# Layer norms that sum their squares on TensorE, and closings that share the low parts of their weights among three engines: one change to a two-block fp32 kernel

## The chip, the cores and the metric

One Trainium2 chip, one of its cores. Five engines work side by side, each through its own queue and in order: TensorE (PE in the profile, its weight loads as PEld), VectorE (DVE), ScalarE (ACT), GpSimd (POOL) and SyncE (SP, which only issues DMAs). The metric is the device time of one execution in microseconds (us). Sequence 512, model width 1024, everything float32.

## The reference

Two blocks of two layers run one after the other. The first block: a convolution module (`conv`) and an FFN (`ffn0`), a sparse attention (`nsa`) and an FFN (`ffn1`). The second: a state-space mixer (`mamba`) and an MLP (`mlp0`), a stick-breaking attention (`sb`) and an MLP (`mlp1`). What the change touches is the layer norm inside the convolution module and the four of the second block:

```python
def layer_norm(x, g, b):
    mu = jnp.mean(xf, axis=-1, keepdims=True)
    var = jnp.mean(jnp.square(xf - mu), axis=-1, keepdims=True)
    return ((xf - mu) * lax.rsqrt(var + LN_EPS) * g + b)
...
h = layer_norm(DEEPNORM_ALPHA * h + mix, ln_mix_g[layer], ln_mix_b[layer])
h = layer_norm(DEEPNORM_ALPHA * h + squared_relu_mlp(h, mlp_w1[layer], mlp_w2[layer]), ...)
```

## The kernel before, in words

Activations lie feature-major: a tile `x[m]` (m = 0 to 7) holds 128 features by 512 tokens. Every float32 product is made of three matmuls (`mm3`, lines 135 to 137): weights and activations are split into a high part that the fast matmul type represents, and a low part, the rest. So each weight that arrives by an SP DMA (`wraw`) has to be split before PE can use it (`w`, lines 108 to 133): ACT writes the high part `whi`, and the low part `wlo` comes in one of three ways, chosen by `c.weng`: a subtraction on DVE (`None`) or on POOL (`nc.gpsimd`), both at line 96, or `"dma"`: ACT writes minus the high part (L122) and a DMA issued from POOL adds the raw weight to it (L123).

Five weight slots are turned over in order: weight n takes the buffers of weight n-5, so it can be loaded and split only when PE is through with that one.

A **closing** (`closing` and `out_halves`) ends `mamba`, `mlp0`, `sb` and `mlp1`. It runs the out-projection twice, over tokens 0 to 255 (half 0) and 256 to 511 (half 1), with eight weights each time. DVE adds each result to `x` (L523) and sums the features (`add`, L312 and L314). The layer norm is `HalfNorm`, once for each half, in three stages:

- `centre`: PE adds up the features over the partitions (L319), DVE subtracts the mean (L323), ACT squares (L328), and DVE adds the squares up in two sums (L329, six adds for a half).
- `stats`: four one-column matmuls (L336) sum each half of 128 tokens over the partitions. DVE turns the sums into 1/sqrt (`rstd_of`, L152 to L162).
- `finish`: PE spreads the result over the partitions (L183, two matmuls). DVE multiplies (L538), ACT adds the bias and writes the high part of the next product's activations (L540), DVE their low part (L543).

The three stages of half 0 are issued among the products of half 1's out-projection; those of half 1 among the first products of the next phase, the `head`: 4 or 5 weights of 128x1024, split at the end of the closing. `mlp1` ends the kernel: it has no head, and its half 1 is a chain with nothing beside it. The convolution's layer norm uses the same class, and its out-projection takes its low parts by turns from DVE and POOL.

In all closings `c.weng` is POOL, for the eight weights of both halves (128x512 in `mamba` and `sb`, 128x1024 in `mlp0` and `mlp1`) and for the head.

The order of the work is not that of the program text. The class `Arrange` takes all instructions, their dependences and a price for each, and lists them greedily: at each step the instruction that can start first, ties by a priority (the table `PRIO` moves some groups up or down). What comes out is the fixed order of each engine's queue. `graph` builds the dependences, `price` and `schedule` hold the costs.

Of the kernel before, what the change touches and what calls it, by code (L numbers as in the profile page):

```python
# [11 lines left out]
AF = mybir.ActivationFunctionType  # L12
OP = mybir.AluOpType
AX = mybir.AxisListType
PSUM = bass.MemoryType.PSUM
P = 128
S = 512
D = 1024
# [277 lines left out]
class HalfNorm:  # L296
# [19 lines left out]
    def centre(self, h):  # L316
        c, nc, cl = self.c, self.c.nc, self.cols(h)
        mu = c.bank()[:, :S // 2]
        nc.tensor.matmul(mu, c.ones, self.tot[h], start=True, stop=True)  # L319
        self.sq = acc = [c.s()[:, :S // 2] for _ in range(2)]  # L320
        for m in range(KT):
            y = self.ys[m][:, cl]
            nc.vector.scalar_tensor_tensor(y, mu, -1.0 / D, y, op0=OP.mult, op1=OP.add)  # L323
            if m < 2:
                nc.scalar.activation(acc[m], y, AF.Square)
            else:
                q = c.s()[:, :S // 2]
                nc.scalar.activation(q, y, AF.Square)  # L328
                nc.vector.tensor_tensor(acc[m % 2], acc[m % 2], q, op=OP.add)  # L329

    def stats(self, h):
        c = self.c
        ps = c.bank()
        for i in range(2):
            for j in range(2):
                c.nc.tensor.matmul(ps[:, i:i + 1], self.sq[j][:, i * P:(i + 1) * P], c.ones[:, :1], start=j == 0, stop=j == 1)  # L336
        self.r[h] = c.rstd_of(ps[:, :2], D, 1e-5)

    def finish(self, h):
        rs = self.c.rstd_spread(self.r[h], self.c.bank)[:, :S // 2]  # L340
# [169 lines left out]
    return [wl_(np.ascontiguousarray(w[a * P:b * P])) for a, b in ((0, 8), (8, 15), (15, 22))]  # L510


def out_halves(c, wname, hs, piece, beside, done=None):

    nc = c.nc
    for h in range(2):
        cl = slice(h * (S // 2), (h + 1) * (S // 2))
        ht = [[t[:, cl] for t in a] for a in hs]
        for m in range(KT):
            wt = c.w(c.ins[wname][piece][m])  # L520
            ps = c.t(c.pmm, [P, S], F32, "mm")[:, :S // 2]
            c.proj(ps, wt, ht)
            nc.vector.tensor_tensor(c.x[m][:, cl], c.x[m][:, cl], ps, op=OP.add)  # L523
            if done is not None:
                done(m, h)
            if (h, m) in beside:
                beside[h, m]()


def closing(c, wname, hs, piece, name, head):  # L530

    nc = c.nc
    c.weng = nc.gpsimd
    xs = c.acts() if head else None

    def apply(m, cl, rs):
        x = c.x[m][:, cl]
        nc.vector.scalar_tensor_tensor(x, x, c.pcol(name + "g", m), rs, op0=OP.mult, op1=OP.mult)  # L538
        if head:
            nc.scalar.activation(xs[0][m][:, cl], x, AF.Identity, bias=c.pcol(name + "b", m))  # L540
        nc.scalar.activation(x, x, AF.Identity, bias=c.pcol(name + "b", m))
        if head:
            nc.vector.tensor_tensor(xs[1][m][:, cl], x, xs[0][m][:, cl].bitcast(F32), op=OP.subtract)  # L543
        else:
            nc.sync.dma_start(c.ins["out"][m][:, cl], x)

    ln = HalfNorm(c, c.x, apply)
    s0, s1 = ln.stages(0), ln.stages(1)
    p = (0, 2, 4) if len(hs[0]) == KT else (0, 5, 7)
    out_halves(c, wname, hs, piece, {(1, m): f for m, f in zip(p, s0)}, ln.add)  # L550
    if not head:
        for f in s1:
            f()
        c.stored = True
        return
    wts = [c.w(src) for src in head]
    c.weng = None
    c.xs, c.head = xs, [c.t(c.pmm, [P, S], F32, "mm") for _ in head]
    for h in range(2):
        cl = ln.cols(h)  # L560
        for js in [(0, 1)] + [(j,) for j in range(2, len(head))]:
            for k in range(KT):
                for j in js:
                    sl = slice(k * P, k * P + P)
                    c.mm3(c.head[j][:, cl], wts[j][0][:, sl], wts[j][1][:, sl], xs[0][k][:, cl], xs[1][k][:, cl],
                          k == 0, k == KT - 1)
                if h == 0 and (js[0], k) in c.hpos:
                    s1.pop(0)()
# [1155 lines left out]
class Arrange:  # L1724
# [11 lines left out]
    def __init__(self, tc, edges=()):  # L1736
        self.tc, self.ins = tc, [i for b in tc.nc.cur_f.blocks if b.name == tc.start_bb_name for i in b.instructions]
        n = len(self.ins)
        self.eng, self.deps, self.touch = [-1] * n, [()] * n, [()] * n
        self.tag, self.bufs, self.count = {}, {}, {}  # L1740
        self.graph()
        at = {i.name: j for j, i in enumerate(self.ins)}
        for a, b in edges:
            self.deps[at[b]] = tuple(set(self.deps[at[b]]) | {at[a]})
        self.cost = [self.price(j) for j in range(n)]
        self.users, self.missing = [[] for _ in range(n)], [0] * n
        for j in range(n):
            for k in self.deps[j]:
                if self.eng[j] >= 0 and self.eng[k] >= 0:
                    self.users[k].append(j)  # L1750
                    self.missing[j] += 1
# [19 lines left out]
    def graph(self):  # L1771
        seen, closed, opened, gate, psum = {}, [], [], {}, set()
        for j, i in enumerate(self.ins):
# [29 lines left out]
            for nm, w, b in here:  # L1803
                d.update(k for k, w2, b2 in seen.get(nm, ()) if (w or w2) and (b2[0] < b[1] and b[0] < b2[1] and b2[2] < b[3] and b[2] < b2[3]
                                                                               or w and w2 and self.eng[j] == self.eng[k] == self.PE))
                if nm in psum:

                    d.update(k for k, w2, b2 in seen.get(nm, ()) if self.eng[j] != self.eng[k] and b2[2] < b[3] and b[2] < b2[3])
                if nm in gate:
                    d.add(gate[nm])  # L1810
            for nm, w, b in here:
# [8 lines left out]
    def price(self, j):  # L1820

        i, e = self.ins[j], self.eng[j]
        if e in (-1, self.GATE):
            return 0, 0, False
        kind = type(i).__name__
        if kind == "InstLoadActFuncSet":
            return 1283, 1283, False
        if kind == "InstDMACopy":
            return (870 if e == self.POOL else 370), 0, False
        size = lambda a: int(np.prod([n for _, n in list(a.ap)[1:]] or [1]))  # L1830
        mem = lambda a: self.tile(a) and ("P" if "PSUM" in str(self.tile(a).space) else "S")
        n = max(size(a) for a in list(i.ins) + list(i.outs) if hasattr(a, "ap"))
        if e == self.PE:
            n = size(i.ins[0])
            if i.is_transpose:
                o = 108
            elif "float32r" in str(i.ins[0].dtype):
                o = max(n / 2.4 + 12.7, 110) + 100 * (list(i.ins[1].ap)[-1][0] == 0)
            else:
                o = 2 * max(n / 1.2 + 12.7, 107)  # L1840
            return o, o + 165, False
        src = [mem(a) for a in i.ins if hasattr(a, "bass_ap") and mem(a) and (size(a) > 1 or n == 1)]
        if e == self.ACT:
            ptr = sum(1 for a in list(i.ins)[1:] if mem(a))
            d = (160 if mem(i.ins[0]) == "P" else 205) + 0.835 * n + (0, 75, 170)[min(ptr, 2)]
            return (d + 60, d + 30, False) if len(i.outs) > 1 else (d - 100, d, False)
        if e == self.DVE:
            fast = kind in ("InstTensorScalarPtr", "InstTensorCopy") and "P" not in src and len(src) < 2
            if kind == "InstMemset":
                d = 58 + 0.83 * n  # L1850
            elif fast:
                d = 150 + 0.54 * n
            elif kind == "InstReciprocal":
                d = 150 + 6.2 * n
            else:
                d = 150 + 1.05 * n + 45 * (kind == "InstTensorScalarPtr" and len(src) > 1 and len(i.ins) > 2)
            return d - 80, d, src.count("S") > 1 or fast
        d = {"InstMemset": 90 + 0.85 * n, "InstTensorScalarAffineSelect": 180 + 0.88 * n, "InstTensorCopy": 180 + 0.84 * n}.get(kind, 190 + 2.17 * n)
        return d - 50, d, kind != "InstMemset"
# [11 lines left out]
    def schedule(self, prio):  # L1871
# [12 lines left out]
        def release(j, end):  # L1884
            todo = [(j, end)]
            while todo:
                j, end = todo.pop()
                for u in self.users[j]:
                    ready[u] = max(ready[u], end + self.hop(self.eng[j], self.eng[u], type(self.ins[u]).__name__ == "InstDMACopy") if self.eng[j] != self.PE or self.eng[u] != self.PE else 0)
                    missing[u] -= 1  # L1890
                    if not missing[u]:
                        if self.eng[u] == self.GATE:
# [22 lines left out]
        for _ in range(sum(0 <= e < 5 for e in self.eng)):  # L1915
# [18 lines left out]
            if e == self.ACT:  # L1934
# [3 lines left out]
                    table = {"ln"}  # L1938
                elif f is not None:
                    if table is None or not table & set(f):  # L1940
                        start, table = start + 1283, set(f)
                    table = table & set(f)
            elif e == self.PE:
                w = int(start // 3413)
# [170 lines left out]
```

## Time and profile before

| what | value |
|---|---|
| median of 3 runs | 2956.26 us (2954.11 to 2956.95) |
| profiled execution | 2953.39 us |
| its span in the trace | 2951.6 us, mean granted PE clock 0.973 |
| HBM read | 246.33 MB, 84 GB/s over the span |

The profiled execution is one run of the program with the hardware profiler on; 1.79 us of it lie outside the span of the trace. It stands 2.87 us under the median of the three runs. Times in the trace count from the start of the span. A matmul of three parts on 256 tokens shows as three records, one for each of L135, L136 and L137; a full float32 matmul, as the one-column ones are, as two records.

### The profile page before, as it was taken

The numbers are of one execution on the slowest core, as the hardware profiler recorded it, in microseconds if no ns is written. First come the engines' busy times: TensorE is split into PE (matmuls) and PEld (weight loads), VectorE is DVE, ScalarE is ACT, GpSimd is POOL, SyncE is SP. The second block draws the span as 40 slices with busy tenths as digits, with TensorE's granted clock in tenths as the row PEclk, the third lists the DMA queues.
The fourth block names the chain that finished last, engine by engine and source line by source line (L and its number), as shares of the span: only waits on it lengthen the run. The fifth ranks groups of instructions, "written<-read, shape, count | busy, mean of one in ns | idle before, by whom it ended". The sixth has DMA issues, their size and how long they took to land.

```text
span 2951.6 us, 38106 instructions
## 1 busy us (share of the span) xinstructions
PE 2808.2 (95%) x14645; PEld 2390.0 (81%) x14645; DVE 1717.2 (58%) x2944; ACT 1489.2 (50%) x2317; POOL 453.1 (15%) x433
## 2 busy tenths in 40 slices
PE   8989999999888899999999999799999999799997
PEld 7878888878777688887788888688888888788887
DVE  8976344546877944444775756743336566743335
ACT  4454222336566632223886877443334788543333
POOL 0010000034222100000111111400015222500004
PEclk9989999998999999999999999899999999899998
DMA  5323323221111122233556564433333444423332
GB/s 189 122 80 124 100 89 103 86 71 53 46 46 45 42 95 93 93 101 105 140 129 143 126 160 107 129 100 100 93 99 115 115 121 91 140 93 94 99 93 93
DMA packets 94789, 300.18 MB, mean 102 GB/s; under 512 B 11216, under 2 KB 13776, under 8 KB 94608
## 3 DMA queue, kind: packets, MB, share of 16 engines
q1 hardware_dynamic: 80064, 253.58, 27.4%
q0 software_dynamic: 14544, 44.18, 7.9%
q8 instruction: 115, 1.88, 0.3%
q14 instruction: 66, 0.54, 0.1%
HBM read 246.33 MB, written 2.10 MB: 84 GB/s over the span
## 4 chain that ended last, share of the span: by engine, by line
PE 59%; ACT 4%; DVE 3%; issue 1%; DMA 1%; POOL 0%; ACTq 0%; POOLq 0%
PE mm L135 17%; PE mm L136 17%; PE mm L137 17%; PE z L1653 1%; PE e L1417 1%; DVE s L329 1%; DMA wlo<-wraw 1%; PE mm L1669 1%; PE e L1384 0%; PE e L1383 0%; ACT th L95 0%; PE mm L1027 0%; PE mm L1041 0%; DVE x L538 0%; ACT whi L121 0%
## 5 line engine op out<-in xcount | busy, mean ns | idle before, releaser
L95 ACT ACTIVATE whi<-wraw 128x1024 fp32r<-128x1024 f32 (+2 forms) x383 | 385.0, 1009 | 994.8 <-PE mm L136 780.4
L135 PE MATMUL mm<-xh,whi 128*128 128x512 f32 (+1 forms) x2240 | 847.8, 383 | 24.8 <-ACT whi L95 12.8
L137 PE MATMUL mm<-xh,wlo 128*128 128x512 f32 (+1 forms) x2240 | 848.9, 380 | 2.3 <-DVE wlo L96 1.4
L136 PE MATMUL mm<-xl,whi 128*128 128x512 f32 (+1 forms) x2240 | 848.8, 381 | 0.9 <-DVE xl L543 0.6
L135 PEld LDWEIGHTS mm<-xh,whi 128*128 128x128 f32 x2240 | 424.0, 191 | 106.4 <-ACT whi L95 15.4
L137 PEld LDWEIGHTS mm<-xh,wlo 128*128 128x128 f32 x2240 | 425.0, 190 | 83.5 <-DVE wlo L96 3.1
L136 PEld LDWEIGHTS mm<-xl,whi 128*128 128x128 f32 x2240 | 425.5, 190 | 79.0 <-DVE xl L543 1.7
L135 PE MATMUL mm<-hh,whi 128*128 128x512 f32 (+1 forms) x1344 | 482.8, 361 | 6.0 <-ACT whi L95 3.2
L137 PE MATMUL mm<-hh,wlo 128*128 128x512 f32 (+1 forms) x1344 | 482.2, 360 | 2.0 <-DMA wlo<-wraw 0.9
L136 PE MATMUL mm<-hl,whi 128*128 128x512 f32 (+1 forms) x1344 | 481.9, 360 | 0.9 <-DVE hl L96 0.9
L96 POOL TENSOR_TENSOR wlo<-wraw,whi 128x1024 fp32r<-128x1024 f32 (+2 forms) x119 | 255.9, 2160 | 1366.8 <-ACT whi L95 1348.8
L96 DVE TENSOR_TENSOR wlo<-wraw,whi 128x1024 fp32r<-128x1024 f32 (+1 forms) x264 | 316.3, 1200 | 183.7 <-ACT whi L95 180.8
L135 PEld LDWEIGHTS mm<-hh,whi 128*128 128x128 f32 x1344 | 255.2, 190 | 44.1 <-ACT hh L95 3.8
L137 PEld LDWEIGHTS mm<-hh,wlo 128*128 128x128 f32 x1344 | 255.1, 190 | 40.1 <-DMA wlo<-wraw 2.1
L136 PEld LDWEIGHTS mm<-hl,whi 128*128 128x128 f32 x1344 | 255.3, 190 | 36.9 <-DVE hl L96 1.4
L287 DVE TENSOR_TENSOR x<-x,mm 128x512 f32<-128x512 f32 x80 | 55.0, 687 | 222.5 <-PE mm L137 222.5
L123 POOL DMA_DIRECT2D wlo<-wraw x101 | 87.8, 870 | 518.7 <-ACT wlo L122 353.9
L121 ACT ACTIVATE whi<-wraw 128x1024 fp32r<-128x1024 f32 (+2 forms) x101 | 92.2, 913 | 87.0 <-PE mm L136 73.7
L96 DVE TENSOR_TENSOR hl<-s,hh 128x512 fp32r<-128x512 f32 (+1 forms) x120 | 88.0, 734 | 77.2 <-ACT hh L95 77.1
L503 DVE TENSOR_TENSOR s<-mm,rstd 128x512 f32<-128x512 f32 x44 | 30.4, 691 | 136.0 <-PE mm L137 136.0
L95 ACT ACTIVATE hh<-s 128x512 fp32r<-128x512 f32 (+1 forms) x120 | 75.8, 632 | 42.1 <-DVE s L504 27.9
L122 ACT ACTIVATE wlo<-wraw 128x1024 fp32r<-128x1024 f32 (+2 forms) x101 | 91.7, 908 | 5.8 <-PE mm L136 5.5
(454 smaller groups left out, 4101.7 us busy)
## 6 DMA issues: line engine op xcount, KB each, us to landing
wraw<-mlp_w SPq DMA_DIRECT2D x144, 512.0 KB
wraw<-ffn_w_in SPq DMA_DIRECT2D x88, 512.0 KB
wlo<-wraw POOLq DMA_DIRECT2D x68, 512.0 KB, 4.8
wraw<-ssm_w_in SPq DMA_DIRECT2D x48, 512.0 KB
wraw<-ffn_w_out SPq DMA_DIRECT2D x32, 448.0 KB
wraw<-conv_taps SPq DMA_DIRECT2D x20, 512.0 KB
wraw<-ssm_w_out SPq DMA_DIRECT2D x40, 256.0 KB
wraw<-conv_w_out SPq DMA_DIRECT2D x16, 512.0 KB
```

Of the source, the lines that this page charges most:

```text
L95: nc.scalar.activation(hi, x, AF.Copy)
L96: (eng or nc.vector).tensor_tensor(lo, x, hi.bitcast(F32), op=OP.subtract)
L121: self.nc.scalar.activation(hi[:, :n], raw[:, :n], AF.Copy)
L122: self.nc.scalar.activation(lo[:, :n], raw[:, :n], AF.Copy, scale=-1.0)
L123: self.nc.gpsimd.dma_start(lo[:, :n], raw[:, :n], accum_op=OP.add)
L135: mm(ps, ah, bh, start=start, stop=False)
L136: mm(ps, ah, bl, start=False, stop=False)
L137: mm(ps, al, bh, start=False, stop=stop)
L287: nc.vector.tensor_tensor(c.x[m], c.x[m], ps, op=OP.add)
L329: nc.vector.tensor_tensor(acc[m % 2], acc[m % 2], q, op=OP.add)
L503: nc.vector.tensor_tensor(u, pu, r, op=OP.mult)
L1417: nc.tensor.matmul(py[:, sl], xds[j][:, q, e2, :], ms[e2][i][:, sl], start=i == 0, stop=i == 1)
```

## The change

- `centre` no longer adds the squares on DVE. Each square (ACT, now L325) goes to its own scratch tile and PE sums it at once: two one-column matmuls for each of the eight features tiles (L328 of the changed kernel), sixteen for a half, which add up in one PSUM bank. `stats` has no matmul left. For ten halves that is 160 one-column matmuls in place of 40, and 60 additions of 128x256 fewer on DVE.
- `LOWS` names, for each closing, where the low parts of half 0, half 1 and the head are made. Counted over the kernel, DVE gets 18 (`mamba`: 8 of 128x512 and 5 of 128x1024; `sb`: 5 of 128x1024), adding DMAs 20 (`mamba` half 0: 8 of 256 KB; `sb` half 1: 8 of 256 KB; `mlp0`'s head: 4 of 512 KB), each with one more copy on ACT, and POOL makes 38 fewer.
- `Arrange` keeps PSUM dependences also between instructions of one engine, without letting them delay a start; prices a table load at 1390 instead of 1283 ns, a broadcast operand of PE 100 ns higher and matmuls of at most 64 partitions twice as high.

```diff
@@ HalfNorm
-        self.sq = acc = [c.s()[:, :S // 2] for _ in range(2)]
+        self.ps = c.bank()
         for m in range(KT):
             y = self.ys[m][:, cl]
             nc.vector.scalar_tensor_tensor(y, mu, -1.0 / D, y, op0=OP.mult, op1=OP.add)
-            if m < 2:
-                nc.scalar.activation(acc[m], y, AF.Square)
-            else:
-                q = c.s()[:, :S // 2]
-                nc.scalar.activation(q, y, AF.Square)
-                nc.vector.tensor_tensor(acc[m % 2], acc[m % 2], q, op=OP.add)
+            q = c.s()[:, :S // 2]
+            nc.scalar.activation(q, y, AF.Square)
+
+            for i in range(2):
+                nc.tensor.matmul(self.ps[:, i:i + 1], q[:, i * P:(i + 1) * P], c.ones[:, :1], start=m == 0 and i == 0, stop=m == KT - 1,
+                                 skip_group_check=True)
 
     def stats(self, h):
-        c = self.c
-        ps = c.bank()
-        for i in range(2):
-            for j in range(2):
-                c.nc.tensor.matmul(ps[:, i:i + 1], self.sq[j][:, i * P:(i + 1) * P], c.ones[:, :1], start=j == 0, stop=j == 1)
-        self.r[h] = c.rstd_of(ps[:, :2], D, 1e-5)
+        self.r[h] = self.c.rstd_of(self.ps[:, :2], D, 1e-5)
...
+LOWS = {"mamba": ("dma", None, None), "sb": ("pool", "dma", None), "mlp0": ("pool", "pool", "dma"), "mlp1": ("pool", "pool", None)}
...
@@ out_halves, for each half h
+        if lows:
+            c.weng = lows[h]
...
@@ closing
-    c.weng = nc.gpsimd
+    lows = [nc.gpsimd if x == "pool" else x for x in LOWS[c.ph]]
...
+    c.weng = lows[2]
     wts = [c.w(src) for src in head]
...
@@ Arrange
-                    d.update(k for k, w2, b2 in seen.get(nm, ()) if self.eng[j] != self.eng[k] and b2[2] < b[3] and b[2] < b2[3])
+                    near = {k for k, w2, b2 in seen.get(nm, ()) if b2[2] < b[3] and b[2] < b2[3]}
+                    self.late.update((k, j) for k in near - d if self.eng[j] == self.eng[k])
+                    d |= near
...
-            return 1283, 1283, False
+            return 1390, 1390, False
...
-                o = max(n / 2.4 + 12.7, 110) + 100 * (list(i.ins[1].ap)[-1][0] == 0)
+                o = max(n / (2.4 if i.ins[0].ap[0][1] > 64 else 1.2) + 12.7, 110) + 200 * (list(i.ins[1].ap)[-1][0] == 0)
```

What moves, in three places. The first is TensorE at the end of `mamba`'s half 1 out-projection (tiles `mm`, inputs `xh`, `xl`), before it the sums of half 0's squares and the spread, after it the head's products. Before:

```order
L136 MATMUL mm_16515<-xl_3087_16085,whi_16511 128x256
L137 MATMUL mm_16515<-xh_3083_16081,wlo_16512 128x256
L336 MATMUL st_16469<-ones,s_16334 128x1
L336 MATMUL st_16469<-ones,s_16335 128x1
L336 MATMUL st_16469<-ones,s_16334 128x1
L336 MATMUL st_16469<-ones,s_16335 128x1
L183 MATMUL st_16530<-ident,rr_16476 128x128 x2
L319 MATMUL st_16606<-acc_16144,ones 128x256
L135 MATMUL mm_16595<-xh_3094_16128,whi_16567 128x256
```

And changed:

```order
L136 MATMUL mm_16541<-xl_3087_16097,whi_16537 128x256
L137 MATMUL mm_16541<-xh_3083_16093,wlo_16538 128x256
L183 MATMUL st_16556<-ident,rr_16502 128x128 x2
L319 MATMUL st_16632<-acc_16156,ones 128x256
L135 MATMUL mm_16621<-xh_3094_16140,whi_16593 128x256
```

The sums of the squares no longer stand at the end of the out-projection: their sixteen matmuls are issued 65 product matmuls earlier. The spread still stands right before the head.

The second place is VectorE there: the end of half 0's 1/sqrt (`rr`), the low parts of the head's weights (`wlo`, 128x1024), the sum of half 1 (`acc`) and half 0's finish (L538 before, L539 changed). Before:

```order
L314 TENSOR_TENSOR acc_16144<-acc_16144,x_7_91 128x256
L156 SCALAR_TENSOR_TENSOR rr_16476<-rsq_16477,rr_16476 128x2
L523 TENSOR_TENSOR x_8_92<-x_8_92,mm_16515 128x256
L314 TENSOR_TENSOR acc_16144<-acc_16144,x_8_92 128x256
L538 SCALAR_TENSOR_TENSOR x_1_85<-x_1_85,par,st_16530 128x256
```

And changed:

```order
L156 SCALAR_TENSOR_TENSOR rr_16502<-rsq_16503,rr_16502 128x2
L520 TENSOR_TENSOR x_6_90<-x_6_90,mm_16485 128x256
L96 TENSOR_TENSOR wlo_16600<-wraw_16597,whi_16599 128x1024
L314 TENSOR_TENSOR acc_16156<-acc_16156,x_6_90 128x256
L520 TENSOR_TENSOR x_7_91<-x_7_91,mm_16520 128x256
L96 TENSOR_TENSOR wlo_16606<-wraw_16603,whi_16605 128x1024
L96 TENSOR_TENSOR wlo_16612<-wraw_16609,whi_16611 128x1024
L96 TENSOR_TENSOR wlo_16618<-wraw_16615,whi_16617 128x1024
L314 TENSOR_TENSOR acc_16156<-acc_16156,x_7_91 128x256
L520 TENSOR_TENSOR x_8_92<-x_8_92,mm_16541 128x256
L539 SCALAR_TENSOR_TENSOR x_1_85<-x_1_85,par,st_16556 128x256
```

Between the 1/sqrt and the first multiplication of the finish now stand four low parts of the head.

The third place is the end of the kernel on TensorE, half 1 of `mlp1`'s layer norm. Before:

```order
L319 MATMUL st_25224<-acc_24619,ones 128x256
L336 MATMUL st_25256<-ones,s_25226 128x1
L336 MATMUL st_25256<-ones,s_25227 128x1
L336 MATMUL st_25256<-ones,s_25226 128x1
L336 MATMUL st_25256<-ones,s_25227 128x1
L183 MATMUL st_25275<-ident,rr_25263 128x128 x2
```

And changed:

```order
L319 MATMUL st_25298<-acc_24687,ones 128x256
L328 MATMUL st_25300<-ones,s_25302 128x1 x2
L328 MATMUL st_25300<-ones,s_25307 128x1 x2
...
L328 MATMUL st_25300<-ones,s_25332 128x1 x2
L328 MATMUL st_25300<-ones,s_25337 128x1 x2
L183 MATMUL st_25355<-ident,rr_25343 128x128 x2
```

Here nothing stands beside the sums, before as after; there are four times as many matmuls in the chain. Elsewhere in `ffn0`, `nsa`, `ffn1` and the bodies of the MLPs and of `sb`, TensorE's order is the same; in `conv` and `mamba` some instructions stand up to 70 places from where they were.

## Rows read from the trace of the kernel before

**Rows 1.** The page: busy time of the engines, and the chain that ended last.
```profile
PE 2808.2 (95%) x14645; PEld 2390.0 (81%) x14645; DVE 1717.2 (58%) x2944; ACT 1489.2 (50%) x2317; POOL 453.1 (15%) x433
...
PE 59%; ACT 4%; DVE 3%; issue 1%; DMA 1%; POOL 0%; ACTq 0%; POOLq 0%
```

**Rows 2.** Waits of PE: waited for; us in total, times, longest us.
```profile
PE st L336 <- DVE s L329: 21.5, 6, 5.6
PE st L183 <- DVE rr L156: 18.2, 5, 5.3
...
PE mm L136 <- DMA wlo<-wraw: 4.0, 1, 4.0
```

**Rows 3.** Stretches: us; busy (records) of PE, PEld, DVE, ACT, POOL; PEclk; DMA; GB/s.
```profile
159.00:182.00 23.00, 12.58 (x81) 10.97 (x80) 12.98 (x42) 7.68 (x17) 0.00 (x0) 0.77 0.00 1
1850.00:1868.00 18.00, 10.20 (x50) 8.99 (x51) 11.47 (x24) 4.63 (x8) 6.91 (x6) 0.72 0.33 87
1884.00:1905.80 21.80, 11.25 (x67) 9.86 (x65) 17.77 (x40) 8.15 (x14) 12.79 (x6) 0.69 0.59 181
2249.00:2290.00 41.00, 34.84 (x248) 33.18 (x247) 34.08 (x87) 21.78 (x49) 11.05 (x6) 0.88 0.23 66
2553.00:2590.00 37.00, 24.78 (x176) 23.56 (x175) 31.59 (x76) 16.68 (x37) 12.90 (x6) 0.77 0.35 112
2905.00:2930.00 25.00, 25.00 (x211) 24.95 (x209) 15.78 (x43) 7.97 (x15) 12.10 (x6) 1.00 0.08 29
2934.50:2951.60 17.10, 3.06 (x12) 2.71 (x12) 9.55 (x33) 6.12 (x16) 0.00 (x0) 0.55 0.18 62
```

**Rows 4.** Timeline, closing of mamba: start, us, engine, line, records, [idle before <- releaser].
```profile
1885.06 12.23 POOL L96 TENSOR_TENSOR wlo<-wraw,whi 128x1024 fp32r<-128x1024 f32 x5 [0.50 <-ACT whi L95]
...
1889.64 5.45 DVE L329 TENSOR_TENSOR s<-s,s 128x256 f32<-128x256 f32 x3 [3.47 <-ACT s L328]
...
1892.66 0.59 PE L336 MATMUL st<-ones,s 128*128 128x1 f32 x2 [2.95 <-DVE s L329]
...
1895.14 1.44 PE L336 MATMUL st<-ones,s 128*128 128x1 f32 x6 [1.89 <-DVE s L329]
...
1901.90 1.22 PE L183 MATMUL st<-ident,rr 128*128 128x128 f32 x4 [5.32 <-DVE rr L156]
```

**Rows 5.** Timeline of TensorE, closing of mlp0.
```profile
2256.74 0.73 PE L336 MATMUL st<-ones,s 128*128 128x1 f32 x6
...
2264.46 1.22 PE L183 MATMUL st<-ident,rr 128*128 128x128 f32 x4 [4.01 <-DVE rr L156]
```

**Rows 6.** Groups by line and shape: busy us, mean ns | idle before.
```profile
L96 DVE TENSOR_TENSOR wlo<-wraw,whi 128x1024 fp32r<-128x1024 f32 x228 | 278.8, 1224 | 181.1 <-ACT whi L95 180.8
...
L329 DVE TENSOR_TENSOR s<-s,s 128x256 f32<-128x256 f32 x60 | 48.7, 852 | 11.4 <-ACT s L328 11.3
...
L523 DVE TENSOR_TENSOR x<-x,mm 128x256 f32<-128x256 f32 x80 | 32.8, 417 | 38.9 <-PE mm L137 38.6
...
L96 DVE TENSOR_TENSOR wlo<-wraw,whi 128x512 fp32r<-128x512 f32 x4 | 2.6, 684 | 0.0
...
L122 ACT ACTIVATE wlo<-wraw 128x512 fp32r<-128x512 f32 x32 | 19.8, 620 | 1.0 <-PE mm L136 0.9
...
L123 POOL DMA_DIRECT2D wlo<-wraw x101 | 87.8, 870 | 518.7 <-ACT wlo L122 353.9 <-DVE x L287 48.7 <-issue 21.0
```

**Rows 7.** Timeline before the closing of mamba: VectorE and TensorE.
```profile
1855.66 0.16 DVE L162 TENSOR_SCALAR rv<-e 128x4 f32<-128x4 f32 x1 [1.15 <-PE e L171]
1855.86 1.03 DVE L152 TENSOR_SCALAR rr<-rv 128x4 int32<-128x4 int32 x1
...
1860.97 2.05 PE L183 MATMUL e<-ident,rr 128*128 128x128 f32 x8 [4.34 <-DVE rr L156]
```

**Rows 8.** Timeline, the end of the kernel.
```profile
2934.30 1.75 DVE L323 SCALAR_TENSOR_TENSOR x<-st,x 128x256 f32<-128x256 f32 x5 [0.85 <-PE st L319]
...
2938.87 1.84 PE L336 MATMUL st<-ones,s 128*128 128x1 f32 x8 [4.60 <-DVE s L329]
```

**Rows 9.** The page, DMA issues: KB each, median us from issue to landing.
```profile
wlo<-wraw POOLq DMA_DIRECT2D x32, 256.0 KB, 3.3
```

More of the change, by code (lines that the diff above doesn't have):

```diff
@@ L510, in ffn_out_layout, with out_halves @@
     return [wl_(np.ascontiguousarray(w[a * P:b * P])) for a, b in ((0, 8), (8, 15), (15, 22))]
-def out_halves(c, wname, hs, piece, beside, done=None):
+def out_halves(c, wname, hs, piece, beside, done=None, lows=None):
     nc = c.nc
@@ L549, in closing @@
     p = (0, 2, 4) if len(hs[0]) == KT else (0, 5, 7)
-    out_halves(c, wname, hs, piece, {(1, m): f for m, f in zip(p, s0)}, ln.add)
+    out_halves(c, wname, hs, piece, {(1, m): f for m, f in zip(p, s0)}, ln.add, lows)
     if not head:
@@ L1739, in __init__ @@
         self.eng, self.deps, self.touch = [-1] * n, [()] * n, [()] * n
-        self.tag, self.bufs, self.count = {}, {}, {}
+        self.tag, self.bufs, self.count, self.late = {}, {}, {}, set()
         self.graph()
@@ L1888, in release @@
                 for u in self.users[j]:
-                    ready[u] = max(ready[u], end + self.hop(self.eng[j], self.eng[u], type(self.ins[u]).__name__ == "InstDMACopy") if self.eng[j] != self.PE or self.eng[u] != self.PE else 0)
+                    if (self.eng[j] != self.PE or self.eng[u] != self.PE) and (j, u) not in self.late:
+                        ready[u] = max(ready[u], end + self.hop(self.eng[j], self.eng[u], type(self.ins[u]).__name__ == "InstDMACopy"))
                     missing[u] -= 1
@@ L1940, in schedule @@
                     if table is None or not table & set(f):
-                        start, table = start + 1283, set(f)
+                        start, table = start + 1390, set(f)
                     table = table & set(f)
```

## The prediction

> **What bounds it.** I read the page first. TensorE is busy for 95% of the span and holds 59% of the chain that ended last [rows 1], so a microsecond counts where TensorE idles or runs slowly, and an instruction added to TensorE counts in full. Next TensorE's waits: six waits for the last addition of squares make 21.5 us and five for the end of the 1/sqrt 18.2 us [rows 2]. These are the layer norms' own chains. Then the stretches, to price what each closing loses. Yardstick: from 2905 to 2930 TensorE is never idle, its granted clock is full (1.00, the 2.4 GHz level), and 211 records take 25.00 us, 0.118 us each [rows 3]. A stretch's records times 0.118 is what it would take undisturbed; the rest is lost, by idling or at a lower clock. So [rows 3]: conv 159 to 182: 23.0 - 81 x 0.118 = 13.4 us lost; mamba 1884 to 1905.8: 21.8 - 67 x 0.118 = 13.9; mlp0 2249 to 2290: 41.0 - 248 x 0.118 = 11.6; sb 2553 to 2590: 37.0 - 176 x 0.118 = 16.1; the end 17.1 - 12 x 0.118 = 15.7.
>
> Last the timeline of mamba's closing, for the cause. POOL makes five low parts of the head without a break from 1885.06 to 1897.3, and in that time three additions L329 on DVE take 5.45 us [rows 4]; the addition L523 of the same size, one input from PSUM, takes 0.417, while L329 means 0.852 over the kernel [rows 6]. DVE operations that read two tiles of SBUF stand still while POOL reads SBUF. TensorE waits 2.95 and 1.89 us for these sums and 5.32 us for the 1/sqrt behind them, and its clock means 0.69 [rows 3, 4].
>
> **The change, part by part.** The sum is made against the profiled execution, 2953.39 us; the median of the runs shown is 2.87 higher, which I add at the end.
>
> *One-column matmuls on TensorE.* Six records take 0.73 us at the full clock [rows 5] and 1.44 us at the half one [rows 4]; eight take 1.84 [rows 8], so one more costs (1.84 - 1.44) / 2 = 0.20 at half clock, and about 0.11 at full. Each half gets 12 matmuls more, 24 records: +2.6 us at full clock, +5 at half. Ten halves: **+26** at full clock, in full on the path wherever products wait behind them. The Trainium skill, "TensorE: Matmul & The Clock Gate", section "Back-to-back issue gap", lets narrow matmuls follow each other after about 25 ns; by that the 240 records would cost 6 us and the forecast below would be 20 us lower. The row says 0.11, and the row decides.
>
> *mamba, before the closing.* Half 0's low parts leave POOL. Next to them L152 took 1.03 us where its neighbour L162 on as few elements takes 0.16, and TensorE waited 4.34 us [rows 7]. Without POOL's low parts that chain is shorter: between 0 and -3.5; I take -2.5, since POOL keeps other work that reads SBUF there.
>
> *mamba, half 0's norm.* 13.9 us are lost. The squares' wait (2.95 + 1.89) goes: their matmuls now stand 65 product matmuls before the end. But DVE takes over 8 low parts of 0.684 and 5 of 1.224 [rows 6], 11.6 us, in a stretch where it was busy 17.77 of 21.80 us [rows 3], and four of the 128x1024 ones, 4.9 us, stand between the 1/sqrt and the finish, for which the head's first product waits. I leave 4.4 us of stall and 1.7 of lost clock, 6.1 of 13.9: -7.8 (bounds: nothing left, -13.9; all left, 0). Squares of two halves +5.2, and 1.2 for a clock that sags behind a run of sixteen one-column matmuls. Mamba in all: -2.5 - 7.8 + 5.2 + 1.2 = **-3.9**.
>
> *mlp0.* Here POOL's low parts of both halves stay; the head's come by adding DMA. 11.6 us are lost. The squares and the spread now stand 72 matmuls (8.5 us) ahead of the head, and those of half 1 36 (4.2 us) ahead of their products, which covers the wait of 4.01 us [rows 5]. I leave 2.5 for the finish and the clock: -9.1 (bounds -11.6 and -4), squares +5.2: **-3.9**.
>
> *sb.* 16.1 us are lost. The spread of half 0 moves some 50 matmuls ahead of its half's mean. DVE gets five low parts of 1.224, 6.1 us, beside half 0's finish, and ACT eight copies of 0.620 [rows 6], 5.0 us, in half 1. I leave 4.3 of stall and 2 of clock: -9.8 (bounds -16.1 and 0), squares +5.2: **-4.6**.
>
> *mlp1.* POOL still makes all its low parts. Half 0: squares +2.6. At the end of the kernel the chain is bare. Before, L323 begins at 2934.30 and the sums end at 2938.87 + 1.84 = 2940.7 [rows 8]. After, two matmuls follow each square, but 32 records at the half clock (mean 0.55 there [rows 3]) are 6.4 us or more, so they end near 2941 too: +0.3. The spread of half 0 stands some 50 matmuls further ahead of half 1's mean, which takes up to 1.5 us of waiting: -1.5. Together **+1.4** (bounds -1 and +4.6).
>
> *conv.* Half 0's chain is bare as well: L329's share goes, the 32 records come at a mean clock of 0.77 [rows 3]: +0.5. Half 1: +2.6, of which 1 is hidden in waits that shrink. **+2.1** (0 to 5).
>
> *Adding DMAs.* Twenty low parts land 3.3 us after issue [rows 9] where POOL takes 12.23 / 5 = 2.4 us for a low part of 128x1024 [rows 4]; the issue is 0.87 us [rows 6] on a POOL that is idle then. In the whole kernel one wait for such a transfer is long, 4.0 us [rows 2], among 101 of them. I take **+1.0** (0 to 12, three places of 4.0). ACT's extra copies in mamba's half 0 cost nothing: 2 x 0.62 us a weight [rows 6] beside 1.4 us of products (12 x 0.118); were they late, it would be TensorE that waits.
>
> *The scheduler's prices and dependences* change order only. Where the order moved without the parts above (conv, mamba) I take 0, with a wait like those of rows 2 (3.6 us in the mean) either way.
>
> **Sum:** -3.9 - 3.9 - 4.6 + 1.4 + 2.1 + 1.0 = -7.9. 2953.4 - 7.9 + 2.9 = **2948.4 us**, 0.27% under the median of before. No change is within 0.2%, 5.9 us, about what a measurement of this kernel can tell.
>
> **The rivals.**
> - *More goes than I leave.* For it: with POOL quiet, DVE has no stretched operations left in mamba and sb, and the low parts may fill gaps. Against: the order puts four low parts ahead of the finish. The 6.1 + 2.5 + 6.3 + 1.2 us that I left vanish: 2932.
> - *DVE becomes the bound*, the low parts taking the place of the locks. For: 17.77 of 21.80 us busy already [rows 3], and 11.6 us more. Against: the lock's time (5.45 us for three additions [rows 4], where five operations of that size take 1.75 at the end [rows 8]) goes. Mamba's 7.8 and sb's 9.8 aren't gained, but the stalls are not longer: +17.6 in all, 2966; 2957 if half of it comes.
> - *Slower: the clock falls behind the one-column matmuls.* TensorE's granted clock is low where it waits and runs one-column matmuls between the waits (0.69 in 1884 to 1905.8, 0.55 at the end [rows 3]). If a run of sixteen takes it down, that half pays 5 instead of 2.6, and the products behind it run at half clock too. Each such run costs 2.4 us or more; from four on (9.6, of which 1.2 is counted) the gain is gone, six give +14.4 - 1.2, 2962, all ten 2971. For: the sixteen stand nearly in one piece in most halves. Against: a run lasts 32 x 0.11 = 3.5 us, with products on both sides, and eight records between products in mlp0 ran at the full clock [rows 5].
> - *The adding DMAs come late*: in each of three places TensorE waits 4.0 us [rows 2]: +11, 2959. The Trainium skill, "SBUF — State Buffer", section "SBUF: two separate sides", says that DVE operations can keep GpSimd from writing a transfer's descriptors; no row here shows it, the issues mean 0.87 us [rows 6].
>
> **Numbers.** Forecast 0.45, more gain 0.18, slower by the clock 0.17, DVE 0.13, late DMAs 0.07. Faster by over 0.2% (under 2950.35): 0.37 of the forecast's 0.45 and the whole 0.18, 0.55. Slower (over 2962.2): 0.12 of the clock's case, 0.04 of DVE's, 0.01 of the DMAs', 0.17. Within: 0.28. The range goes from the second case's 2932 to 2962, which leaves out the clock's worse half and little below. The forecast's own range is 2942 to 2954.
>
> **What would show it.** No wait of TensorE for a sum of squares in mamba, mlp0 and sb; L183's wait in mamba and sb shorter, but a wait for `xh` of some 4 us in its place; L329 gone and no DVE operation of 128x256 over 1 us in mamba and sb; 320 records L328 at about 0.11 us. I am wrong if these wait as long as before, if PEclk is under 0.9 behind the runs of L328, or if waits for `wlo` by DMA exceed 5 us in all.

## The result, and the profile after

The changed kernel takes 2975.53 us (median; 2972.77 to 2977.35) against 2955.64 for the kernel before in the same comparison: a ratio of 1.0064, interval 1.0049 to 1.0079. It is slower by 20 us, 0.6%, where 8 us less were forecast; the range ended at 2962. The profiled execution has a span of 2972.2 us, 20.6 more than before.

The page after, TensorE and the chain, answers to [rows 1]:

```profile
PE 2854.3 (96%) x14885; PEld 2436.3 (82%) x14885; DVE 1680.6 (57%) x2902; ACT 1500.8 (50%) x2337; POOL 401.9 (14%) x415
...
PE 58%; ACT 3%; DMA 3%; DVE 2%; issue 2%; POOL 0%; ACTq 0%; POOLq 0%; SPq 0%; DVEq 0%
```

TensorE is busy 46.1 us longer (2854.3 against 2808.2), with 240 records more. 34.0 us of it are the records that sum the squares; the groups by shape, before and after:

```profile
L336 PE MATMUL st<-ones,s 128*128 128x1 f32 x80 | 13.9, 281 | 21.5 <-DVE s L329 21.5
L328 PE MATMUL st<-ones,s 128*128 128x1 f32 x320 | 47.9, 276 | 2.9 <-ACT s L325 2.9
```

POOL and DVE have lost work, as meant. TensorE's waits after, against [rows 2]:

```profile
PE st L319 <- DVE acc L314: 7.4, 5, 3.9
...
PE mm L137 <- DMA wlo<-wraw: 7.3, 7, 3.3
...
PE st L183 <- DVE rr L156: 4.4, 2, 2.2
...
PE mm L136 <- DMA wlo<-wraw: 3.8, 1, 3.8
...
PE st L328 <- ACT s L325: 2.9, 3, 1.0
```

Two waits of before, to be held against the first two of these:

```profile
PE st L319 <- DVE acc L314: 3.0, 2, 1.5
...
PE mm L137 <- DMA wlo<-wraw: 0.9, 2, 0.7
```

The 21.5 us of waiting for the squares' additions are gone (2.9 for the squares themselves came in their place), and of the 18.2 for the 1/sqrt 4.4 are left: 39.7 us became 7.3. Other waits grew: for the mean's sum (L319) from 3.0 to 7.4 us, for low parts by DMA from 4.9 to 11.1. In all TensorE idles 117.9 us (2972.2 - 2854.3) where it idled 143.4 (2951.6 - 2808.2). So 25.5 us of stall went and the kernel is slower all the same: the loss lies in TensorE's busy time, in its added records and in its clock. The timeline shows it. This is TensorE behind half 0's squares in `mlp0`, sixteen one-column matmuls in one piece:

```profile
2255.09 4.22 PE L328 MATMUL st<-ones,s 128*128 128x1 f32 x32
2259.17 0.56 PE L136 MATMUL mm<-hl,whi 128*128 128x256 f32 x1
2259.53 0.41 PE L137 MATMUL mm<-hh,wlo 128*128 128x256 f32 x1
2259.74 0.41 PE L135 MATMUL mm<-hh,whi 128*128 128x256 f32 x1
2259.96 0.41 PE L136 MATMUL mm<-hl,whi 128*128 128x256 f32 x1
2260.17 0.41 PE L137 MATMUL mm<-hh,wlo 128*128 128x256 f32 x1
```

The 32 records take 4.22 us, 0.13 each: the first follow each other at 0.11 us, the last at 0.21. Behind them the products follow each other at 0.21 us instead of 0.12 (the undisturbed 0.118 of [rows 3]), until 2264.9. TensorE has not waited at all here; it only ran one-column matmuls before its granted clock fell. The same stretch with the granted clock (columns as in [rows 3]):

```profile
2255.00:2265.00 10.00, 10.00 (x63) 10.00 (x62) 5.57 (x19) 3.49 (x8) 3.60 (x2) 0.66 0.33 106
```

63 records in 10.00 us, at a mean clock of 0.66. At the full clock it would have been 85.

At the end of the kernel, against [rows 8]:

```profile
2953.31 2.74 DVE L323 SCALAR_TENSOR_TENSOR x<-st,x 128x256 f32<-128x256 f32 x8 [0.85 <-PE st L319]
...
2954.30 6.96 PE L328 MATMUL st<-ones,s 128*128 128x1 f32 x32 [1.03 <-ACT s L325]
```

From the start of L323 to the end of the sums 7.95 us pass (2953.31 to 2961.26), before 6.4 (2934.30 to 2940.7): 32 records at half clock.

By places: each trace has 12063 records of the three-part products, and the table gives the time between the same two of them, counted from the first (and, last, to the end of the span), in us:

| stretch | before | after | no squares | 64 columns | 128 columns | doubled |
|---|---|---|---|---|---|---|
| conv's layer norm | 53.8 | 59.0 | 54.2 | 55.7 | 52.6 | 74.1 |
| closing of mamba | 51.1 | 53.4 | 48.8 | 49.9 | 50.5 | 70.4 |
| closing of mlp0 | 53.5 | 51.9 | 45.3 | 47.4 | 47.4 | 63.9 |
| closing of sb | 43.3 | 47.0 | 44.8 | 43.7 | 43.9 | 58.8 |
| closing of mlp1, end | 43.4 | 47.2 | 43.4 | 44.9 | 43.6 | 63.0 |
| these five | 245.0 | 258.6 | 236.5 | 241.7 | 238.1 | 330.2 |
| everything else | 2706.6 | 2713.6 | 2701.7 | 2710.6 | 2710.7 | 2714.4 |

The five norms got 13.6 us longer and the rest 7.0. (The last four columns are the runs below.)

### The profile page after: what moved, and what is told of

Same layout as the page of the kernel before. It is cut to its first block, busy times and chain, and to the rows that moved or that the text cites. A ratio compares the mean times of both kernels' runs of the same rounds, so it can differ in the third digit from the quotient of the medians.

```text
span 2972.2 us, 38558 instructions
## 1 busy us (share of the span) xinstructions
PE 2854.3 (96%) x14885; PEld 2436.3 (82%) x14885; DVE 1680.6 (57%) x2902; ACT 1500.8 (50%) x2337; POOL 401.9 (14%) x415
## 4 chain that ended last, share of the span: by engine, by line
PE 58%; ACT 3%; DMA 3%; DVE 2%; issue 2%; POOL 0%; ACTq 0%; POOLq 0%; SPq 0%; DVEq 0%
PE mm L137 17%; PE mm L136 17%; PE mm L135 17%; DMA wlo<-wraw 2%; PE z L1655 1%; PE st L328 1%; PE e L1419 1%; PE mm L1671 1%; PE e L1386 0%; PE e L1385 0%; ACT th L95 0%; PE mm L1043 0%; ACT whi L121 0%; DMA wraw<-ssm_w_out 0%; PE mm L1029 0%
## 5 line engine op out<-in xcount | busy, mean ns | idle before, releaser
L96 DVE TENSOR_TENSOR wlo<-wraw,whi 128x1024 fp32r<-128x1024 f32 (+2 forms) x282 | 333.8, 1186 | 190.0 <-ACT whi L95 186.9
L96 POOL TENSOR_TENSOR wlo<-wraw,whi 128x1024 fp32r<-128x1024 f32 (+2 forms) x81 | 187.0, 2315 | 1405.3 <-ACT whi L95 1328.0
L123 POOL DMA_DIRECT2D wlo<-wraw x121 | 105.4, 882 | 565.8 <-ACT wlo L122 444.9
L122 ACT ACTIVATE wlo<-wraw 128x1024 fp32r<-128x1024 f32 (+2 forms) x121 | 105.5, 873 | 7.4 <-PE mm L136 7.0
```

The lines of the kernel that those rows point to most:

```text
L96: (eng or nc.vector).tensor_tensor(lo, x, hi.bitcast(F32), op=OP.subtract)
L122: self.nc.scalar.activation(lo[:, :n], raw[:, :n], AF.Copy, scale=-1.0)
L123: self.nc.gpsimd.dma_start(lo[:, :n], raw[:, :n], accum_op=OP.add)
```

## The experiments

Three theories of what costs the 20 us. A: the one-column matmuls cost their records and then the clock behind them. B: the new low parts cost. C: the order that `Arrange` makes costs.

**Take the parts apart.** First, without the squares on TensorE, LOWS and Arrange as changed:

```diff
-        self.ps = c.bank()
+        self.sq = acc = [c.s()[:, :S // 2] for _ in range(2)]
...
+                nc.vector.tensor_tensor(acc[m % 2], acc[m % 2], q, op=OP.add)
```

> The change without its first part: the squares are added on DVE and summed by four one-column matmuls a half, as before; LOWS and Arrange as changed. Theory A (the one-column matmuls cost their records, 26 us over ten halves, and then the products behind each run go at half clock for a while, some 2 us each, so about 45 us in all, of which the stalls that went give back less): this one is faster than the kernel before, 2930 to 2942 us, and 33 to 45 us faster than the changed kernel. Theory B (the new low parts are what costs: DMA waits and DVE's five low parts ahead of the finish): this one is as slow as the changed kernel, 2965 to 2980. Theory C (the order that Arrange makes is what costs): also 2965 or more.

Measured: 2941.83 us, ratio 0.995 (0.9938 to 0.9962); 33.7 less than the changed kernel, with LOWS and Arrange as there. As the main cause theories B and C fall. TensorE's waits there:

```profile
PE st L336 <- DVE s L329: 9.8, 3, 4.6
...
PE st L319 <- DVE acc L314: 8.9, 5, 4.2
...
PE st L183 <- DVE rr L156: 7.5, 4, 2.2
```

and VectorE's additions, in the groups by shape:

```profile
L329 DVE TENSOR_TENSOR s<-s,s 128x256 f32<-128x256 f32 x60 | 29.2, 529 | 12.9 <-ACT s L328 12.7
```

With part of the low parts moved off POOL and the squares still on DVE, L329 means 0.529 us instead of 0.852 [rows 6], the squares' wait falls from 21.5 to 9.8 us and that for the 1/sqrt from 18.2 to 7.5 [rows 2]. More than half of these two waits (22.4 of 39.7 us) goes without the squares on TensorE; 5.9 of it comes back in the wait for the mean's sum (8.9 where it was 3.0). The Trainium skill, "SBUF — State Buffer", section "SBUF: two separate sides", has it that a DVE operation with two SBUF inputs and a GpSimd operation that reads SBUF shut each other out for a whole instruction; the trace agrees, 0.852 against 0.529 us.

Second, without LOWS (POOL makes all the low parts of the closings, the head's too):

```diff
-LOWS = {"mamba": ("dma", None, None), "sb": ("pool", "dma", None), "mlp0": ("pool", "pool", "dma"), "mlp1": ("pool", "pool", None)}
+LOWS = {p: ("pool", "pool", "pool") for p in ("mamba", "sb", "mlp0", "mlp1")}
```

> The change without its second part: POOL makes all low parts of the closings; squares on PE and Arrange as changed. Theory A: the squares' 45 us stay, and of the closings' stalls only the wait for the last addition goes (some 20 us); DVE is still stretched by POOL: 2970 to 2985 us. Theory B: the cost goes with LOWS: 2945 to 2956. Theory C: 2970 or more, which A tells too; the run without both parts settles that.

Measured: 2982.35 us, ratio 1.0086 (1.0074 to 1.0098). The cost stays and the gain of LOWS is missing; the wait for the 1/sqrt is back:

```profile
PE st L183 <- DVE rr L156: 17.8, 4, 7.2
```

Third, neither part, only `Arrange` (both edits above together).

> Neither squares on PE nor LOWS: only Arrange's dependences and prices are changed. Theories A and B: within 4 us of the kernel before, 2952 to 2960. Theory C: slower by most of the 20 us, 2965 to 2976.

Measured: 2960.25 us, ratio 1.0015 (1.0006 to 1.0024), 3.4 us slower than before. So, in medians: Arrange alone +3.4; LOWS on top of it -18.4 (to 2941.83), squares on top of it +22.1 (to 2982.35), both +15.3. The squares cost 33.7 beside LOWS and 22.1 without it, since without it they still save a wait that LOWS removes too: the wait for the squares' additions is 21.5 us without LOWS and 9.8 with it. Fourth, POOL in place of the adding DMAs in LOWS, the rest as changed:

```diff
-LOWS = {"mamba": ("dma", None, None), "sb": ("pool", "dma", None), "mlp0": ("pool", "pool", "dma"), "mlp1": ("pool", "pool", None)}
+LOWS = {"mamba": ("pool", None, None), "sb": ("pool", "pool", None), "mlp0": ("pool", "pool", "pool"), "mlp1": ("pool", "pool", None)}
```

> The changed kernel with POOL in place of the adding DMAs in LOWS (mamba half 0, sb half 1, mlp0's head); DVE keeps its 18 low parts. Theory A: the waits of PE for low parts by DMA were 11.1 us in the changed kernel against 4.9 before; without the 20 transfers 5 to 6 us of waiting and 1 to 2 of clock go, and some 2 us come back where POOL stretches DVE again: 2968 to 2974. Theory B: most of the loss goes, 2955 to 2962.

Measured: 2971.76 us, ratio 1.0047 (1.0035 to 1.0059), 3.8 less than the changed kernel; the two intervals overlap, so the difference is not certain. TensorE's waits for low parts by DMA there:

```profile
PE mm L136 <- DMA wlo<-wraw: 4.0, 1, 4.0
PE mm L137 <- DMA wlo<-wraw: 3.9, 2, 3.3
```

The 7.3 us of the second row after are 3.9 here, so 3.4 us were waits for the new transfers; the other 3.9 aren't theirs, since this kernel hasn't got those transfers.

**Is it the clock?** The same kernel with the same order on every engine, but each one-column matmul streams 64 equal columns:

```diff
-                nc.tensor.matmul(self.ps[:, i:i + 1], q[:, i * P:(i + 1) * P], c.ones[:, :1], start=m == 0 and i == 0, stop=m == KT - 1,
+                nc.tensor.matmul(self.ps[:, i * 64:(i + 1) * 64], q[:, i * P:(i + 1) * P], c.ones[:, :64], start=m == 0 and i == 0, stop=m == KT - 1,
...
-        self.r[h] = self.c.rstd_of(self.ps[:, :2], D, 1e-5)
+        self.r[h] = self.c.rstd_of(self.ps[:, :128:64], D, 1e-5)
```

> The changed kernel, same order on every engine, but each matmul that sums a square streams 64 equal columns instead of one into the PSUM bank (the 1/sqrt reads columns 0 and 64). Theory A1 (besides its records, a run of one-column matmuls lets the granted clock fall, and the products behind it pay): the records stay at about 0.11 us, the clock stays up behind the runs, and 10 to 20 us come back: 2956 to 2966 us; half-clock stretches behind L328 go. Theory A2 (only the number of records costs, the clock's stretches are chance or come from elsewhere): 2973 to 2980, the same stretches.

Measured: 2957.07 us, ratio 0.9996 (0.9986 to 1.0006). More work at the same places, and 18.5 us less. The run in `mlp0` and what follows it:

```profile
2246.06 3.73 PE L328 MATMUL st<-ones,s 128*128 128x64 f32 x32
2249.60 0.36 PE L136 MATMUL mm<-hl,whi 128*128 128x256 f32 x1
2249.80 0.28 PE L137 MATMUL mm<-hh,wlo 128*128 128x256 f32 x1
2249.92 0.29 PE L135 MATMUL mm<-hh,whi 128*128 128x256 f32 x1
```

and the stretch, to be held against the row of 2255 to 2265 above:

```profile
2246.00:2256.00 10.00, 10.00 (x87) 10.00 (x87) 5.06 (x21) 4.52 (x9) 4.98 (x3) 1.00 0.36 108
```

87 records instead of 63, the clock at 1.00. The granted clock fell where TensorE ran without a pause but with one column to a matmul, and didn't where each had 64; the 63 columns more cost nothing in the run itself. Over the kernel, nine of the ten runs of L328 have the half clock in them or right behind them; with 64 columns three do, and each of these three has 1 us or more of waiting in it or just before it.

The tenth run of the changed kernel is half 0 of `mlp1`, where the scheduler set 19 product records among the 32:

```profile
2928.41 1.22 PE L328 MATMUL st<-ones,s 128*128 128x1 f32 x10
2929.49 0.36 PE L136 MATMUL mm<-hl,whi 128*128 128x256 f32 x1
2929.69 0.28 PE L328 MATMUL st<-ones,s 128*128 128x1 f32 x2
...
2928.00:2943.00 15.00, 15.00 (x130) 15.00 (x130) 10.08 (x26) 4.82 (x10) 7.17 (x3) 1.00 0.01 1
```

The last row is the stretch with the granted clock: it stayed at 1.00. This is one place that came about by the order; setting products among the squares everywhere was not tried.

With 128 columns:

> As before with 128 columns: the spread's matmuls of 128 columns take 0.15 us a record at full clock (four in 0.60), so 320 records cost 12 us more than at 0.11. Theory A1: the clock stays up as with 64, so some 8 to 15 us slower than with 64 columns, 2966 to 2978. Theory A2: 2985 to 2992.

Measured: 2950.3 us, ratio 0.9984 (0.9975 to 0.9993). The expectation that 128 columns cost more than 64 was wrong: the run takes 3.78 us instead of 3.73. With 64 columns the order of every engine is that of the changed kernel; with 128 some records of TensorE stand elsewhere in the closings of `conv`, `mamba` and `sb`, so the 6.8 us between the two need not be the columns'.

```profile
2244.54 3.78 PE L328 MATMUL st<-ones,s 128*128 128x128 f32 x32
```

The cost doubled: each one-column matmul twice, the second to columns that nobody reads.

```diff
+                nc.tensor.matmul(self.ps[:, 2 + i:3 + i], q[:, i * P:(i + 1) * P], c.ones[:, :1], start=False, stop=m == KT - 1,
+                                 skip_group_check=True)
```

> The changed kernel with each one-column matmul issued twice (the second goes to spare columns of the bank that nobody reads). The suspected cost doubled: theory A2 says 320 records more at 0.11 us, +35: 3008 to 3014. Theory A1: the runs of 7 us end at half clock themselves, so half of the added records cost 0.21, and the products behind pay as before or longer: +50 to +75, 3025 to 3050. If the records were hidden beside other work: under 2990.

Measured: 3043.89 us, ratio 1.0296 (1.0282 to 1.031), 68.4 more than the changed kernel where the records alone would be 35. In the run in `mlp0` the second half shows the half clock in the matmuls themselves (L328 and, as L330, its double):

```profile
2289.84 0.32 PE L328 MATMUL st<-ones,s 128*128 128x1 f32 x2
2290.02 0.36 PE L330 MATMUL st<-ones,s 128*128 128x1 f32 x2
...
2298.22 0.56 PE L328 MATMUL st<-ones,s 128*128 128x1 f32 x2
2298.65 0.57 PE L330 MATMUL st<-ones,s 128*128 128x1 f32 x2
```

**What is left without the squares.** The kernel before with LOWS alone, Arrange as it was:

> The kernel before with LOWS alone: no matmuls for squares, no change in Arrange. The run without squares gave 2941.8, Arrange alone costs 3.4 (2960.25 against 2956.86). If the parts add, 2936 to 2941, the fastest so far; if LOWS needs Arrange's new order, 2942 to 2950.

Measured: 2943.17 us, ratio 0.9952 (0.9939 to 0.9966). The parts don't add: Arrange's 3.4 didn't come off (2943.17 without its changes, 2941.83 with them; the intervals overlap). And the same with POOL in place of the adding DMAs:

> The kernel before with LOWS alone, POOL in place of its adding DMAs: only DVE's 18 low parts are new. LOWS alone gave 2943.17. If the DMAs cost what they cost in the changed kernel: 2938 to 2942; if DVE is stretched by POOL again in the additions of squares, which are back here: 2943 to 2950.

Measured: 2946.28 us, ratio 0.9961 (0.9949 to 0.9975). The two are not told apart by their intervals.

**The squares another way.** ACT writes each square in the fast matmul type, TensorE streams its 256 columns against a tile of ones (one record), and the sums stand on all partitions. DVE then takes the 1/sqrt on 128x256, and the spread isn't needed. The sum of squares so has the fast type's rounding:

```diff
-            q = c.s()[:, :S // 2]
+            q = c.t(c.sc, [P, S], F32R, "s")[:, :S // 2]
...
-            for i in range(2):
-                nc.tensor.matmul(self.ps[:, i:i + 1], q[:, i * P:(i + 1) * P], c.ones[:, :1], start=m == 0 and i == 0, stop=m == KT - 1,
-                                 skip_group_check=True)
+            nc.tensor.matmul(self.ps[:, :S // 2], c.onesr, q, start=m == 0, stop=m == KT - 1)
...
-        rs = self.c.rstd_spread(self.r[h], self.c.bank)[:, :S // 2]
+        rs = self.r[h]
```

> The changed kernel with the squares summed another way: the squares are written in the fast matmul type and stream 256 columns at a time against a tile of ones, 8 matmuls a half of one record each (80 in place of 160 of two records); the sums then stand on all partitions, so the 1/sqrt is taken on 128x256 by DVE (10 operations at some 0.42 us instead of 0.16) and the spread falls away. Theory A: 80 records at 0.12 us are 10 us where 320 at 0.11 were 35, and the clock stays up as with 128 columns; against the 2950.3 of that run some 25 to 35 us of records and 6 of the spread go, and the longer 1/sqrt, 2.6 us more in each of ten halves, costs at most 5 to 15 where nothing covers it: 2920 to 2938, the fastest. If the 1/sqrt on DVE is on the path everywhere: 2940 to 2950.

Measured: 2935.71 us, ratio 0.9928 (0.9915 to 0.994), the fastest kernel here, 21.5 us under the one before in the same comparison (2957.24). In `mlp0` a square's matmul now is one among the products, at their pitch:

```profile
2234.53 0.33 PE L328 MATMUL st<-s,onesr 128*128 128x256 f32 x1
2234.69 0.28 PE L138 MATMUL mm<-hl,whi 128*128 128x256 f32 x1
2234.81 0.28 PE L139 MATMUL mm<-hh,wlo 128*128 128x256 f32 x1
2234.93 0.28 PE L137 MATMUL mm<-hh,whi 128*128 128x256 f32 x1
2235.04 0.28 PE L328 MATMUL st<-s,onesr 128*128 128x256 f32 x1
```

By the count of the table above the five norms take 228.1 us here, and the rest 2705.0. With POOL for the adding DMAs:

> The same with POOL in place of the 20 adding DMAs. With one-column matmuls that was 3.8 us faster than the changed kernel (2971.76 against 2975.53), so 2 to 6 us faster than the run before this one; if POOL stretches the 1/sqrt on DVE, whose operands now all lie in SBUF, up to 10 slower.

Measured: 2946.44 us, ratio 0.9961 (0.9948 to 0.9973). Here the medians are 10.7 us apart in favour of the DMAs, where 2 to 6 the other way had been the first expectation; the two traces are 6.1 apart. By the count of the table none of that lies in the five norms. Half is in the products ahead of `mamba`'s closing (127.3 against 124.2 us), where POOL makes the low parts again, and half in `nsa`, which LOWS doesn't touch. That POOL's stretching of DVE is why was not shown.

## Why the prediction was wrong

**The step that failed** is the term "One-column matmuls on TensorE": "+2.6 us at full clock ... Ten halves: +26 at full clock", with 1.2 us for a sagging clock in one place. The price at the full clock held: 24 added records at 0.117 us (3.73 / 32, with 64 columns at the full clock) are 2.8 us a half. What was missing is the half clock in the runs and behind them: the 240 added records took 34.0 us (47.9 - 13.9) and not 26, and the products behind them slowed too. 64 columns in place of one, everything else alike, gave back 18.5 us, 128 columns, with some records moved, 25.2. That leaves 2957.07 and 2950.3, 8.7 and 1.9 us above the forecast. I had this as a rival, with the right mechanism and a low price: "each such run costs 2.4 us or more ... all ten 2971". Measured are 2975.53, and in the 10 us from the start of `mlp0`'s run (87 - 63) x 0.115 = 2.8 us are lost. My argument against it, that a run of 3.5 us has products on both sides and that eight records had run at the full clock between products, did not hold: eight don't show what 32 do. The half-clock rows of before, [rows 4] and [rows 8], stood behind waits, so they could not tell one-column matmuls from idling.

The mean granted clocks give an estimate of the size. It is 0.971 after, so 2972.2 x 0.029 = 86.2 us of the span's clock are missing; 2951.6 x 0.027 = 79.7 before (0.973), and 2952.3 x 0.023 = 67.9 with 64 columns (0.977). Between one column and 64 that is 18.3 us. Against before it is only 6.5: the half clock that went with the stalls came back behind the squares.

Two of the signs of being wrong that the prediction named are there: a clock under 0.9 behind a run of L328 (0.66), and waits for `wlo` by DMA over 5 us in all (11.1, though 4.9 of that was there before). Nor did all 320 records take about 0.11 us: 47.9 / 320 is 0.15.

**What the forecast did not ask** is what each part of the change wins alone. LOWS by itself removes 11.7 of the 21.5 us of waiting for the squares (9.8 left) and 10.7 of the 18.2 for the 1/sqrt. Beside it the squares on TensorE could win only the rest, and they cost their records and the clock. The sum doesn't count a stall twice, so this is not where its miss comes from; but a price for each part alone could have shown that the squares cost more than they win beside LOWS (33.7 us).

Point by point: *mamba* -3.9 was forecast for before and in the closing; the closing alone went +2.3 (51.1 to 53.4). Of the 2.5 ahead of it 1.7 came (the 440 product records ahead of the table's stretch take 124.9 us instead of 126.6), but not by the wait that I meant. L152 takes 0.17 us instead of 1.03, yet DVE now puts other operations into that chain, and TensorE waits 4.64 us where it waited 4.34 [rows 7]:

```profile
1873.22 2.05 PE L183 MATMUL e<-ident,rr 128*128 128x128 f32 x8 [4.64 <-DVE rr L156]
```

In the closing the four low parts ahead of the finish cost what I gave them; TensorE's next matmul waits for the last sum behind them 3.9 us where I had left 4.4:

```profile
1907.97 3.49 DVE L96 TENSOR_TENSOR wlo<-wraw,whi 128x1024 fp32r<-128x1024 f32 x3
...
1913.00 0.91 PE L319 MATMUL st<-acc,ones 128*128 128x256 f32 x2 [3.89 <-DVE acc L314]
```

It is the mean of half 1 that waits, not `xh` of the head. *mlp0* -3.9: -1.6. *sb* -4.6: +3.7. *mlp1* +1.4: +3.8. *conv* +2.1: +5.2. In every closing the sign of the miss is the same, 2.3 to 8.3 us too low, two halves each (for `mamba` against the -1.4 of the closing alone); with 64 columns the five come to 241.7 instead of 258.6. *Adding DMAs* +1.0: 3.8 by the run without them (its interval overlaps that of the changed kernel), inside the bounds. *The scheduler's order* 0: alone it cost 3.4 us, inside the 3.6 that I had allowed. In the changed kernel the rest of the kernel got 7.0 us longer, which I did not foresee. Some 5 of it are one place in `mamba`'s body:

```profile
1749.36 0.73 PE L137 MATMUL mm<-xh,wlo 128*128 128x512 f32 x1 [3.32 <-DMA wlo<-wraw]
```

This is a transfer that the kernel before has too. TensorE waits at the same record in the run without the squares and in the one with Arrange's changes alone:

```profile
1735.18 0.50 PE L137 MATMUL mm<-xh,wlo 128*128 128x512 f32 x1 [2.04 <-DMA wlo<-wraw]
1735.90 0.50 PE L137 MATMUL mm<-xh,wlo 128*128 128x512 f32 x1 [1.67 <-DMA wlo<-wraw]
```

The kernel before and the two with LOWS alone, whose Arrange is the old one, have no wait there. So it goes with Arrange's changes; why it is longer with the squares (3.32), and which instruction moved it, was not tried. The remaining 2 us or so lie mainly in `nsa`, where no part of the change is: between the records that stand at 630 and 1045 us before, 414.5 us before and 417.8 after. In the runs of the table this stretch takes 411.7 to 421.4, and I leave it open.

## What to carry to other kernels

A matmul with one column costs as much of TensorE's time as one with 128 (0.12 us a record) and, where sixteen of them stood in one piece, the clock of the products behind it too. Here the clock came to 18.5 to 25.2 us beside 28 us (240 x 0.117) for the added records, so price such a run at 1.7 to 1.9 times its own time. Or give each matmul columns (64 cost nothing more here), or turn it round so that the data streams and the ones stay (2935.71). Before adding up what two parts of a change remove, ask of each what the other leaves of that stall. Where DVE is stretched by POOL, moving POOL's work away gained 18.4 us here, and moving DVE's to TensorE, which is the bound, cost 22.1.

## What the runs showed of the hardware that I had not expected

TensorE's granted clock went to half, the 1.2 GHz level (0.66 in the mean over 10 us, 63 records instead of 87), without any idle time, behind 32 one-column records, and stayed at 1.00 with 64 columns in each at nearly the same pace. The Trainium skill, "TensorE: Matmul & The Clock Gate", section "HAM oscillation — how this bites in real kernels", puts the rule as one against idle gaps of TensorE; here the clock fell in a stretch where TensorE was busy for 10.00 of 10.00 us, so the rule by itself would have forecast no fall.

A record takes the same time with 1, 64 and 128 columns: 0.73 / 6 = 0.12 us [rows 5], 3.73 / 32 = 0.117 and 3.78 / 32 = 0.118. I had expected 0.15 with 128, from four of the spread's that take 0.60.
